# An encoder trunk on one core: the last two up-projection groups of the MLP behind each other, then eight pieces of the down projection

## The chip, the cores and the metric

One core of a Trainium2 chip runs the kernel. The core has TensorE (PE in the profile, with PEld for the loading of weights into it), VectorE (DVE), ScalarE (ACT), GpSimd (POOL) and SyncE (SP), each with its own queue of instructions, which it works off in order. SP issues nearly all DMAs of this kernel. The metric is the device time of one execution in microseconds, as the median over several runs; the profile is of one further execution.

## The reference

Two layers, each with a token mixer and a gated MLP over 256 tokens of width 1024, and a last normalisation. The change touches the MLP alone, whose inner width is 2816, that is 22 chunks of 128 channels:

```python
def _conv_ffn(xn, w_up, conv_w, conv_b, w_down):
    a, gval = jnp.split(xn @ w_up, 2, axis=-1)
    a = lax.conv_general_dilated(a, conv_w[:, None, :], window_strides=(1,),
                                 padding=((CONV_WIDTH // 2, CONV_WIDTH // 2),),
                                 dimension_numbers=('NWC', 'WIO', 'NWC'),
                                 feature_group_count=D_FF) + conv_b
    return (jax.nn.gelu(a) * gval) @ w_down

h = h + _conv_ffn(_rmsnorm(h, norm2[layer]), w_up[layer], conv_w[layer], conv_b[layer], w_down[layer])
```

Branch a is projected, convolved over three tokens for each channel and put through gelu; branch g is projected and multiplied with it; the product goes through the down projection and is added to the residual h.

## The kernel before, in words

**Precision.** Every float32 operand is split into a high and a low part. A weight arrives from memory as a 1 MB load (`raw`, three buffers), and each load holds two pieces. Of each piece ACT makes the high part (`wh`, line 219, a cast) and DVE the low part (`wl`, line 221, a subtraction). A product then takes three matmuls: high by high, high by low, low by high. The class `Weights` hands out the pieces in the order in which they were registered, loads ahead and splits three pieces ahead; `wh` and `wl` have five buffers, so a piece is split only when an older one has been used up by PE.

**The MLP.** Chunks 0 to 19 are projected in groups of four: group `("a", n)` or `("g", n)` is 512 columns of one branch, four pieces, 48 matmuls (`by_tokens`, line 680, tiles `t_ps`). Its result has the tokens on the partitions. `cross` turns it so that the channels lie there: DVE transposes blocks (line 724), SP stores to DRAM (line 726) and reads back with four DMAs (line 731) into `zga` or `zg`. The four reads wait on SP for the store, and what SP has behind them waits too. `z_of` holds two groups of each branch.

`up(f)` finishes a chunk: ACT copies it (line 1277), ACT starts the convolution (1286), DVE adds the two neighbours (1287, 1290), ACT takes gelu (1299), DVE multiplies with branch g (1301), ACT casts the product to the high part `actq` (1310) and DVE subtracts for the low part `actk` (1311). Chunks 20 and 21, the last two, go another way: `proj` (line 556, tiles `proj_ps`) projects them with the channels on the partitions, two pieces at a time, and `add_up` (lines 592, 593) adds the two halves out of PSUM, so that they need no crossing.

**The down projection** (`residual_mm`, lines 598 to 600, tiles `res_ps`) takes one piece of weights and one chunk at a time and adds up in four PSUM tiles. Its last four chunks, 18 to 21, are held: their pieces are fetched but their matmuls run last, output segment by output segment, so that the norm behind can begin on the first segment while the others are still computed. In the last layer (`whole`) the last segment has its residual added ahead, by DVE in line 633.

**The order.** `MLP_STEPS` gives the order of the steps and with it that of the weights: a1, g1, d0, a2, g2, d4, a3, g3, d8, a4, g4, d12, p, d16, d20, behind a0 and g0. Step `("d", n)` is the down projection of four chunks from n on, `("p", 20)` the projection of chunks 20 and 21. `CHUNKS_BEHIND` says which chunks `up` is called for behind each half of a step. Within this order a scheduler places the instructions of each engine as their operands allow, with `issue_after` as a lower bound in some places. `half_steps` runs a step by halves; in step p it calls `up`, which itself calls `proj`.

The tail is thus: p with its two chunks, chunks 17 and 18 behind its first half, chunk 19 behind its second, then d16 and d20, the held matmuls, and behind them the norm of the next layer or the output.

Of the kernel before, what the change touches and what calls it, by code (L numbers as in the profile page):

```python
# [27 lines left out]
NF = DFF // P  # L28
# [10 lines left out]
NQ = NF // 4  # L39


def _mlp_steps():


    steps = []
    for n in range(1, NQ):
        steps += [("a", n), ("g", n), ("d", 4 * n - 4)]
    last = 4 * NQ
    steps.append(("p", last))
    return steps + [("d", f) for f in (last - 4, last)]  # L50


MLP_STEPS = _mlp_steps()
CHUNKS_BEHIND = {
    ("a", 1): ((), (0, 1)), ("g", 1): ((2, 3), ()),
    **{("d", 4 * n): ((), (4 * n + 4,)) for n in range(NQ - 1)},
    **{("a", n): ((4 * n - 3,), (4 * n - 2,)) for n in range(2, NQ)},
    **{("g", n): ((4 * n - 1,), ()) for n in range(2, NQ)},
    ("p", 4 * NQ): ((4 * NQ - 3, 4 * NQ - 2), (4 * NQ - 1,)),
}  # L60
HALVES = (slice(0, 512), slice(512, D))
SEGMENTS = (HALVES, (slice(0, 512), slice(512, 768), slice(768, D)))

# [196 lines left out]
def encoder(ctx, tc, x, w_in, w_pool, pool_scale, w_a, w_b, w_o, norm1, norm2, w_up, conv_w,  # L260
# [13 lines left out]
    def cols(w, c0):  # L274

        src = w[:, c0 : c0 + 256].rearrange("(k p) c -> p k c", p=P)
        return W.add(
            src, (8, 256), [((lambda t, j=j: t[:, :, j * P : (j + 1) * P]), (8, P)) for j in (0, 1)]
        )
# [11 lines left out]
    for l in range(DEPTH):  # L291
        for g in range(NG):
            c0 = C_V + g * 512
            slots = (("m2", 0, 2), ("m2", 1, 2), ("ybig",), ("at2",)) if g == 0 else ()
            for j in range(2):
                tag = "k1" if l == 0 and g == 1 and j == 0 else None
                W.use(rows(w_in[l], j * 512, 4, c0, 512, tag), slots[2 * j : 2 * j + 2])
        if l == 0:
            W.n_scaled = len(W.pieces)
        for c in range(3, -1, -1):  # L300
            W.use(cols(w_in[l], c * 256))
        for n, c in enumerate(PAIRS):
            pool = ([], [])
            if n == 1:
                pool = W.add(
                    w_pool[l].rearrange("g (k p) c -> p (g k) c", p=P), (8, 256),
                    [((lambda t, j=j: t[:, 4 * j : 4 * j + 4, :]), (4, 256)) for j in range(2)],
                )
                pool = (pool[:1], pool[1:])
            W.use(pool[0] + cols(w_in[l], C_Q + c * 256))  # L310
            W.use(pool[1] + cols(w_in[l], C_K + c * 256))
        for w, c0 in ((w_a[l], 0), (w_in[l], C_GP)):
            for c in (c0, c0 + 512):
                W.use(rows(w, 0, 4, c, 512) + rows(w, 512, 4, c, 512))
        for c in (0, 512):
            W.use(rows(w_in[l], 0, 4, C_GA + c, 512) + rows(w_in[l], 512, 4, C_GA + c, 512))
            W.use(rows(w_b[l], 0, 4, c, 512))
        for c in range(4):
            W.use(rows(w_o[l], c * 256))
        first_up.append((len(W.pieces), len(W.loads)))  # L320
        slots = (("v1",), ("ybig",), ("at2",))
        for j in range(2):
            tag = None if j else "k1"
            W.use(rows(w_up[l], j * 512, 4, 0, 512, tag), slots[2 * j : 2 * j + 2])
        for j in range(2):
            W.use(rows(w_up[l], j * 512, 4, DFF, 512))
        for kind, n in MLP_STEPS:
            if kind == "p":
                (a0, a1), (g0, g1) = (cols(w_up[l], c + n * P) for c in (0, DFF))
                W.use([a0, g0, a1, g1])  # L330
            elif kind == "d":
                for f in range(n, min(n + 4, NF), 2):
                    W.use(rows(w_down[l], f * P))
            else:
                for j in range(2):
                    W.use(rows(w_up[l], j * 512, 4, (kind == "g") * DFF + n * 512, 512))
# [227 lines left out]
    def proj(x2, n=1):  # L564


        if not ready:
            pieces = [W.get() for _ in range(n)]
            ps = [mmp.tile([P, 2, S], F32, tag="mm", name="proj_ps") for _ in range(n)]
            two_sums(  # L570
                x2, KD,
                *(
                    (b, lambda k, wh=wh: wh[:, k, :], lambda k, wl=wl: wl[:, k, :])
                    for b, (_, (wh, wl)) in zip(ps, pieces)
                ),
            )
            for i, _ in pieces:
                W.free(i)
            ready.extend((b[:, 0], b[:, 1]) for b in ps)
        return ready.pop(0)  # L580

    def halves(a):

        return a.rearrange("p (t m) -> p t m", t=2)

    def in_order(a):

        return a.rearrange("p (m t) -> p t m", t=2)

    def add_up(out, sums):  # L590

        nc.scalar.copy(out=out, in_=sums[1])
        nc.vector.tensor_add(out=out, in0=sums[0], in1=out)
# [322 lines left out]
    for l in range(DEPTH):  # L916
# [21 lines left out]
        if l == 0:  # L938
            with tc.manual_schedule():
                begun = begin_values_of_x()  # L940
            x2 = first_values(*begun, keep_values)
# [24 lines left out]
        for gi in range(3, -1, -1):  # L966
# [10 lines left out]
            cur, n = u, S + 2 * PAD  # L977
# [108 lines left out]
        def weigh(hh):  # L1086
# [20 lines left out]
        steps = {  # L1107
            0: ((scores, 0), (start_turn, 0)),
            2: ((scores, 1), (start_turn, 1)),
            3: ((turn, 0),),  # L1110
            4: ((weigh, 0),),
            6: ((turn, 1), (scores, 2), (start_turn, 2)),
            7: ((weigh, 1),),
            8: ((scores, 3), (start_turn, 3)),
            12: ((turn, 2),),
# [101 lines left out]
        x2 = two_parts("x", "x2")  # L1217
# [21 lines left out]
            ]  # L1239
            for tag in "qk"  # L1240
        )
        acts = {}

# [27 lines left out]
        def up(f):  # L1273
            w0, w1, w2, b = (prm[:, l, j * NF + f : j * NF + f + 1] for j in range(4))
            a = sm.tile([P, S], F32, tag="u", name="a")
            if f < 4 * NQ:
                nc.scalar.copy(
                    out=a.rearrange("p (a j t) -> p t a j", t=2, j=32),
                    in_=of_chunk(z_of["a", f // 4], f % 4),
                )  # L1280
            else:
                sums = proj(x2, 2)
                with W.after_splits():
                    add_up(in_order(a), [halves(b) for b in sums])
            y = sm.tile([P, S], F32, tag="s", name="y")
            nc.scalar.activation(y, a, AF.Identity, bias=b, scale=w1)  # L1286
            nc.vector.scalar_tensor_tensor(  # L1287
                out=y[:, 1:], in0=a[:, : S - 1], scalar=w0, in1=y[:, 1:], op0=ALU.mult, op1=ALU.add
            )
            nc.vector.scalar_tensor_tensor(  # L1290
                out=y[:, : S - 1], in0=a[:, 1:], scalar=w2, in1=y[:, : S - 1],
                op0=ALU.mult, op1=ALU.add,
            )
            g = sm.tile([P, 2, P], F32, tag="p", bufs=3, name="g")
            if f >= 4 * NQ:
                add_up(g, [halves(a) for a in proj(x2, 2)])

            y2 = sm.tile([P, S], F32, tag="us", name="y2")
            nc.scalar.activation(y2, y, AF.Gelu_apprx_tanh)
            if f < 4 * NQ:  # L1300
                nc.vector.tensor_mul(  # L1301
                    out=g.rearrange("p t (a j) -> p t a j", j=32),
                    in0=y2.rearrange("p (a j t) -> p t a j", t=2, j=32),
                    in1=of_chunk(z_of["g", f // 4], f % 4),
                )
            else:
                nc.vector.tensor_mul(out=g, in0=in_order(y2), in1=g)
            n = f % NH
            ah, al = (x[n >= HPG][:, n - HPG * (n >= HPG)] for x in (acth, actl))
            nc.scalar.copy(out=ah, in_=g)  # L1310
            nc.vector.tensor_sub(out=al, in0=g, in1=ah.bitcast(F32))  # L1311
            acts[f] = (ah, al)
# [16 lines left out]
        def half_steps(kind, n):  # L1329
            if kind == "p":  # L1330
                for f in (n, n + 1):
                    up(f)
                    yield
            elif kind == "d":
                for _ in range(n, min(n + 4, NF), 2):
                    next(down)
                    next(down)
                    yield
            else:
                yield from by_halves(kind, n)  # L1340

        for at in MLP_STEPS:
            if at[0] == "d" and at[1] == 4 * NQ:
                break
            chunks = CHUNKS_BEHIND.get(at, ((), ()))
            for _, some in zip(half_steps(*at), chunks):
                for f in some:
                    up(f)
        if l + 1 < DEPTH:
            x2 = two_parts("x", "x2")  # L1350
# [34 lines left out]
```

## Time and profile before

| what | value |
|---|---|
| median of three runs | 870.12 us (869.45 to 870.21) |
| profiled execution | 872.57 us |
| its span, from first to last instruction | 870.8 us |
| PE busy | 856.6 us, 98% |
| PEld, DVE, ACT busy | 724.2, 619.9, 492.3 us |
| DMA moved | 195.17 MB, mean 224 GB/s |

A row of the timeline gives the start in us from the span's start, the duration, the engine, the line, the operation, the tiles (out<-in), the shape and a count; in brackets stands the idle time ahead of it and what ended it. Matmuls are pipelined: a row of 0.39 us is the way of one matmul through the array, and what it costs is the distance to the next start. A row of the waits gives who waited for whom, the sum in us, the number of times and the longest. A row of the groups gives the count, the busy time in all and the mean of one in ns, then the idle time before. Lines are those of the kernel before.

### The profile page before, as it was taken

What the parts mean: (1) busy time and instruction counts of PE and PEld (TensorE: products, weight loads), DVE (VectorE), ACT (ScalarE), POOL (GpSimd) and SP (SyncE); (2) the same over time, 40 slices, a digit from 0 to 9 for tenths busy, and PEclk for the clock granted to TensorE, in tenths of its full rate; (3) what the DMA queues carried; (4) which work ended last, traced back from release to release, by engine and by line L of the source; (5) the groups of instructions that cost most, each with busy time, mean ns of one, the idle gap of its engine ahead of it and who ended that gap; (6) DMA issues with size and microseconds to landing.
All of it is one profiled execution on the core that took longest, in us unless ns stands there. A gap on an engine that the chain in (4) does not pass through costs nothing.

```text
span 870.8 us, 11486 instructions
## 1 busy us (share of the span) xinstructions
PE 856.6 (98%) x4215; PEld 724.2 (83%) x4215; DVE 619.9 (71%) x930; ACT 492.3 (57%) x770; POOL 34.5 (4%) x98
## 2 busy tenths in 40 slices
PE   9999999999999999999899999999999999999996
PEld 8888888888888888888688888988888888888874
DVE  7998785557676777675865987765666777767664
ACT  7656575555455646555645676664544466646462
POOL 1800000000010000000000000000000000000000
PEclk9999999999999999999999999999999999999998
DMA  9676566775736788696626565747875578778631
GB/s 337 205 251 199 189 201 212 265 257 197 267 124 227 257 268 312 221 323 213 233 97 218 170 215 177 240 143 248 307 238 196 165 271 274 268 263 295 228 145 48
DMA packets 139071, 195.17 MB, mean 224 GB/s; under 512 B 6200, under 2 KB 80640, under 8 KB 139016
## 3 DMA queue, kind: packets, MB, share of 16 engines
q1 hardware_dynamic: 138856, 194.18, 65.9%
q8 instruction: 33, 0.54, 0.2%
q10 hardware_dynamic: 160, 0.27, 0.1%
q14 instruction: 22, 0.18, 0.1%
HBM read 176.58 MB, written 17.85 MB: 223 GB/s over the span
## 4 chain that ended last, share of the span: by engine, by line
PE 91%; DVE 3%; DMA 3%; ACT 2%; issue 1%; SPq 0%; POOL 0%; POOLq 0%; ACTq 0%
PE t_ps L680 38%; PE proj_ps L556 22%; PE v_ps L680 6%; PE res_ps L598 5%; PE res_ps L600 5%; PE res_ps L599 5%; PE v_ps L908 3%; DVE wl L221 2%; PE v_ps L815 1%; PE pool_ps L556 1%; DMA crossing<-crossing 1%; PE o_ps L1096 1%; PE s_ps L1047 1%; DMA raw<-in_w_up_dram 1%; PE s_ps L1042 1%; PE o_ps L1092 1%
## 5 line engine op out<-in xcount | busy, mean ns | idle before, releaser
L221 DVE TENSOR_TENSOR wl<-raw,wh 128x1024 fp32r<-128x1024 f32 x274 | 330.2, 1220 | 134.7 <-ACT wh L219 117.7
L219 ACT CAST wh<-raw 128x1024 fp32r<-128x1024 f32 x274 | 283.1, 1049 | 142.1 <-PE t_ps L680 81.5
L680 PE MATMUL t_ps<-wh,x 128*128 128x512 f32 x832 | 259.0, 390 | 0.0
L680 PEld LDWEIGHTS t_ps<-wh,x 128*128 128x128 f32 x832 | 156.2, 188 | 32.3
L680 PE MATMUL t_ps<-wl,x 128*128 128x512 f32 x416 | 161.9, 389 | 0.1
L556 PE MATMUL proj_ps<-x,wh 128*128 128x512 f32 x576 | 136.5, 390 | 0.0
L556 PEld LDWEIGHTS proj_ps<-x,wh 128*128 128x128 f32 x576 | 106.6, 188 | 21.2
L680 PEld LDWEIGHTS t_ps<-wl,x 128*128 128x128 f32 x416 | 78.1, 188 | 16.7 <-DVE wl L221 0.5
L598 PE MATMUL res_ps<-wh,actq 128*128 128x512 f32 (+1 forms) x184 | 71.1, 395 | 7.1 <-ACT actq L1310 4.4
L556 PE MATMUL proj_ps<-x,wl 128*128 128x256 f32 x576 | 74.9, 283 | 0.0
L556 PEld LDWEIGHTS proj_ps<-x,wl 128*128 128x128 f32 x576 | 72.8, 191 | 1.9
L599 PE MATMUL res_ps<-wl,actq 128*128 128x512 f32 (+1 forms) x184 | 71.7, 390 | 0.0
L600 PE MATMUL res_ps<-wh,actk 128*128 128x512 f32 (+1 forms) x184 | 71.0, 390 | 0.0
L598 PEld LDWEIGHTS res_ps<-wh,actq 128*128 128x128 f32 x184 | 35.6, 194 | 16.1 <-ACT actq L1310 6.3
L600 PEld LDWEIGHTS res_ps<-wh,actk 128*128 128x128 f32 x184 | 35.6, 194 | 7.4 <-DVE actk L1311 0.2
L599 PEld LDWEIGHTS res_ps<-wl,actq 128*128 128x128 f32 x184 | 35.7, 194 | 6.9
L680 PE MATMUL t_ps<-wh,po 128*128 128x512 f32 x128 | 41.4, 395 | 0.0
L1310 ACT CAST actq<-g 128x256 fp32r<-128x256 f32 x44 | 17.4, 400 | 29.7 <-DVE g L1301 28.3
L468 POOL TENSOR_SCALAR ss<-ss 128x1 f32<-128x1 f32 x8 | 1.9, 238 | 792.4 <-ACT junk L461 792.4
L724 DVE STREAM_TRANSPOSE crossing<-t_ps 128x512 f32<-128x512 f32 x36 | 24.4, 701 | 9.8 <-PE t_ps L680 9.8
L1287 DVE SCALAR_TENSOR_TENSOR y<-a,prm,y 128x255 f32<-128x255 f32 x44 | 20.6, 477 | 11.0 <-ACT y L1286 11.0
L680 PEld LDWEIGHTS t_ps<-wh,po 128*128 128x128 f32 x128 | 24.0, 188 | 4.9
(203 smaller groups left out, 1080.6 us busy)
## 6 DMA issues: line engine op xcount, KB each, us to landing
raw<-in_w_in_dram SPq DMA_DIRECT2D x58, 1024.0 KB, 5.8
raw<-in_w_up_dram SPq DMA_DIRECT2D x44, 1024.0 KB, 5.3
raw<-in_w_down_dram SPq DMA_DIRECT2D x22, 1024.0 KB, 5.3
crossing<-crossing SPq DMA_DIRECT2D x20, 512.0 KB, 4.8
raw<-in_w_a_dram SPq DMA_DIRECT2D x8, 1024.0 KB, 6.1
raw<-in_w_o_dram SPq DMA_DIRECT2D x8, 1024.0 KB, 4.7
zga<-crossing SPq DMA_DIRECT2D x40, 128.0 KB, 2.6
zg<-crossing SPq DMA_DIRECT2D x40, 128.0 KB, 2.7
```

Of the source, the lines that this page charges most:

```text
L219: inst = nc.scalar.copy(out=h, in_=src)
L221: inst = nc.vector.tensor_sub(out=l, in0=src, in1=h.bitcast(F32))
L556: nc.tensor.matmul(out, w(k), x, start=(steps is first and k == 0), stop=(steps is last and k == nk - 1), skip_group_check=turns["rest"],)
L598: nc.tensor.matmul(ps, ah, wh, start=first, stop=False, skip_group_check=on)
L599: nc.tensor.matmul(ps, ah, wl, start=False, stop=False, skip_group_check=on)
L600: nc.tensor.matmul(ps, al, wh, start=False, stop=last, skip_group_check=on)
L680: nc.tensor.matmul(ps, x2[:, 2 * n + j, part, t, :], w[:, j, :], start=(n + m == 0), stop=(n == last and m == 5),)
L724: nc.vector.transpose(out=y[:, t].rearrange("p q c j -> p c q j"), in_=rows[t])
L815: return nc.tensor.matmul(ps[t], a[:, k, t, :], w[:, k % 2, :], start=first, stop=last)
L908: nc.tensor.matmul(ps[t], a[:, k, t, :], w[:, j, :], start=(k + m == 0), stop=(k == KD - 1 and m == 2),)
L1287: nc.vector.scalar_tensor_tensor(out=y[:, 1:], in0=a[:, : S - 1], scalar=w0, in1=y[:, 1:], op0=ALU.mult, op1=ALU.add)
L1310: nc.scalar.copy(out=ah, in_=g)
```

## The change

The list of steps is written out, each with the chunks behind its two halves. Step d8 moves from between g3 and a4 to behind g4, so a3, g3, a4 and g4 run directly behind each other, and d8 and d12, eight pieces of the down projection, follow. The chunks keep their ascending order, and now the last two come last: 12 behind a4, 13 and 14 with g4, 15 and 16 with d8, 17 and 18 with d12, 19 and 20 behind the first half of p and 21 behind its second. For that, the projection of chunks 20 and 21 is taken out of `up`: step p computes `sums[f]` (two tiles of PSUM for each chunk), and `up` reads them later. All else, the number of instructions of each kind among it, stays.

```diff
-MLP_STEPS = _mlp_steps()
-CHUNKS_BEHIND = {
-    ("a", 1): ((), (0, 1)), ("g", 1): ((2, 3), ()),
-    **{("d", 4 * n): ((), (4 * n + 4,)) for n in range(NQ - 1)},
-    **{("a", n): ((4 * n - 3,), (4 * n - 2,)) for n in range(2, NQ)},
-    **{("g", n): ((4 * n - 1,), ()) for n in range(2, NQ)},
-    ("p", 4 * NQ): ((4 * NQ - 3, 4 * NQ - 2), (4 * NQ - 1,)),
-}
+MLP_STEPS = (
+    ("a", 1, ((), (0, 1))), ("g", 1, ((2, 3), ())),
+    ("d", 0, ((), (4,))), ("a", 2, ((5,), (6,))), ("g", 2, ((7,), ())),
+    ("d", 4, ((), (8,))), ("a", 3, ((9,), (10,))), ("g", 3, ((11,), ())),
+    ("a", 4, ((), (12,))), ("g", 4, ((13,), (14,))),
+    ("d", 8, ((15,), (16,))), ("d", 12, ((17,), (18,))),
+    ("p", 20, ((19, 20), (21,))), ("d", 16, None), ("d", 20, None),
+)
...
             else:
-                sums = proj(x2, 2)
                 with W.after_splits():
-                    add_up(in_order(a), [halves(b) for b in sums])
+                    add_up(in_order(a), [halves(b) for b in sums[f][0]])
...
             if f >= 4 * NQ:
-                add_up(g, [halves(a) for a in proj(x2, 2)])
+                add_up(g, [halves(b) for b in sums[f][1]])
...
             if kind == "p":
                 for f in (n, n + 1):
-                    up(f)
+                    sums[f] = proj(x2, 2), proj(x2, 2)
                     yield
...
-        for at in MLP_STEPS:
-            if at[0] == "d" and at[1] == 4 * NQ:
+        for kind, n, chunks in MLP_STEPS:
+            if chunks is None:
                 break
-            chunks = CHUNKS_BEHIND.get(at, ((), ()))
-            for _, some in zip(half_steps(*at), chunks):
+            for _, some in zip(half_steps(kind, n), chunks):
                 for f in some:
                     up(f)
```

More of the change, by code (lines that the diff above doesn't have):

```diff
@@ L39 @@
 NQ = NF // 4
[L42 to L50, printed above, removed]
-MLP_STEPS = _mlp_steps()
-CHUNKS_BEHIND = {
-    ("a", 1): ((), (0, 1)), ("g", 1): ((2, 3), ()),
-    **{("d", 4 * n): ((), (4 * n + 4,)) for n in range(NQ - 1)},
-    **{("a", n): ((4 * n - 3,), (4 * n - 2,)) for n in range(2, NQ)},
-    **{("g", n): ((4 * n - 1,), ()) for n in range(2, NQ)},
-    ("p", 4 * NQ): ((4 * NQ - 3, 4 * NQ - 2), (4 * NQ - 1,)),
-}
+MLP_STEPS = (
[6 rows of a table added]
+)
 HALVES = (slice(0, 512), slice(512, D))
@@ L326, in encoder @@
             W.use(rows(w_up[l], j * 512, 4, DFF, 512))
-        for kind, n in MLP_STEPS:
+        for kind, n, _ in MLP_STEPS:
             if kind == "p":
@@ L1241, in encoder @@
         )
-        acts = {}
+        acts, sums = {}, {}
         zg = big.tile([P, 2, 8, 4, 32], F32, tag="v1", name="zg")
@@ L1331, in half_steps @@
                 for f in (n, n + 1):
-                    up(f)
+                    sums[f] = proj(x2, 2), proj(x2, 2)
                     yield
             elif kind == "d":
-                for _ in range(n, min(n + 4, NF), 2):
+                for _ in range(2):
                     next(down)
```

## The prediction

> **What bounds the kernel now.** I read the page first, then PE's waits, then PE's instructions in order of time in the two places where it waits.
>
> ```profile
> span 870.8 us, 11486 instructions
> PE 856.6 (98%) x4215; PEld 724.2 (83%) x4215; DVE 619.9 (71%) x930; ACT 492.3 (57%) x770; POOL 34.5 (4%) x98
> ```
>
> PE is busy for 98% of the span, so nothing but its own holes and its own clock can be won. The change leaves the matmuls as they are. The waits say where the holes lie:
>
> ```profile
> PE res_ps L598 <- ACT actq L1310: 4.4, 5, 3.1
> PE res_ps L598 <- DVE res_ps L633: 2.6, 1, 2.6
> ```
>
> These 7.0 us are the down projection waiting for the last chunks' activations (L1310) and, in the last layer, for a DVE add (L633) queued behind them. PE's timeline, the tail of the first layer and then of the last:
>
> ```profile
> 414.70 0.39 PE L600 MATMUL res_ps<-wh,actk 128*128 128x512 f32 x1
> 415.44 0.50 PE L598 MATMUL res_ps<-wh,actq 128*128 128x512 f32 x1 [0.34 <-ACT actq L1310]
> ...
> 418.11 0.40 PE L600 MATMUL res_ps<-wh,actk 128*128 128x512 f32 x1
> 418.81 0.50 PE L598 MATMUL res_ps<-wh,actq 128*128 128x512 f32 x1 [0.30 <-ACT actq L1310]
> ...
> 421.25 0.28 PE L600 MATMUL res_ps<-wh,actk 128*128 128x256 f32 x1
> 424.59 0.50 PE L598 MATMUL res_ps<-wh,actq 128*128 128x512 f32 x1 [3.06 <-ACT actq L1310]
> ```
>
> ```profile
> 843.43 0.39 PE L600 MATMUL res_ps<-wh,actk 128*128 128x512 f32 x1
> 844.16 0.50 PE L598 MATMUL res_ps<-wh,actq 128*128 128x512 f32 x1 [0.34 <-ACT actq L1310]
> ...
> 846.78 0.39 PE L600 MATMUL res_ps<-wh,actk 128*128 128x512 f32 x1
> 847.54 0.50 PE L598 MATMUL res_ps<-wh,actq 128*128 128x512 f32 x1 [0.37 <-ACT actq L1310]
> ...
> 849.03 0.89 PE L600 MATMUL res_ps<-wh,actk 128*128 128x512 f32 x3
> 852.57 1.01 PE L598 MATMUL res_ps<-wh,actq 128*128 128x256 f32 x2 [2.64 <-DVE res_ps L633]
> ```
>
> Each long hole is followed by matmuls at a lower granted clock (the columns of the windows are the stretch, its length, busy time of PE, PEld, DVE, ACT, POOL, granted clock, DMA share, GB/s):
>
> ```profile
> 424.60:429.00 4.40, 4.40 (x12) 3.48 (x13) 4.12 (x5) 1.94 (x2) 0.00 (x0) 0.61 0.97 310
> 852.50:859.10 6.60, 6.53 (x16) 5.21 (x17) 1.82 (x4) 0.83 (x3) 0.22 (x1) 0.52 0.00 0
> ```
>
> The undisturbed pace is read from the chain of waits:
>
> ```profile
> 259.37 21.77 PE t_ps L680 x96
> ...
> 335.96 21.76 PE t_ps L680 x96
> 368.60 21.76 PE t_ps L680 x96
> 401.24 5.57 PE proj_ps L556 x32
> ```
>
> 96 matmuls in 21.76 us are 0.227 us each; one piece of weights (12 matmuls) takes 2.72, one group of a branch (4 pieces) 10.9. A 256-column matmul takes half, 0.12.
>
> **What the holes cost.** From start to start, less the pace. First layer: 0.74 - 0.23 = 0.51; 0.70 - 0.23 = 0.47; 3.34 - 0.12 = 3.22; then 12 matmuls in 4.40 instead of 2.72, 1.68. Together 5.9 us. Last layer: 0.50; 0.53; 3.54 - 0.68 = 2.86; then 14 matmuls of 512 and two of 256 in 6.60 instead of 3.41, 3.2. Together 7.1 us. All 13.0 us come from one cause: ACT and DVE do five chunks (20, 17, 18, 21, 19) while PE has only eight pieces' worth of matmuls to run, the four of step p and d16's two, before it asks for 18 to 21.
>
> The page of the Trainium skill "TensorE: Matmul & The Clock Gate" (section "What's actually happening") says that after an idle window of about 3.4 us the array runs at half rate until it has been busy for one such window. By it each long hole would cost an estimated 1.7 us of slow matmuls, 3.4 in all, and the forecast would end 1.5 us higher; here holes of 3.06 and of only 2.64 us brought the clock down to 0.61 and 0.52, and the slow stretch cost 1.7 once and 3.2 once, so the rows decide.
>
> **The change, part by part.** In each layer the 48 matmuls of d8, with four casts, four subtractions and two 1 MB loads, go behind groups a4 and g4. PE's sum is unchanged. POOL sees nothing. On SP the two loads move past the two loads each of a4 and g4 and past g3's issues; a4's crossing (one store, four reads back) now follows g3's by one group, not two, and d8's and d12's loads stand between or behind the crossings.
>
> Chunks: as built, the queues of ACT and DVE take chunks 12 to 15 as one batch during a4 and g4, 16 to 19 as one batch during d8 and d12. So 17, 18 and 19, which are now done during p and d16, are finished before p begins, hidden beside eight pieces of matmuls (21.8 us). Only 20 and 21 are left for p and the tail.
>
> Tail, counted from p's start, by these group rows of the page:
>
> ```profile
> L221 DVE TENSOR_TENSOR wl<-raw,wh 128x1024 fp32r<-128x1024 f32 x274 | 330.2, 1220 | 134.7 <-ACT wh L219 117.7
> L219 ACT CAST wh<-raw 128x1024 fp32r<-128x1024 f32 x274 | 283.1, 1049 | 142.1 <-PE t_ps L680 81.5
> ...
> L1310 ACT CAST actq<-g 128x256 fp32r<-128x256 f32 x44 | 17.4, 400 | 29.7 <-DVE g L1301 28.3
> ...
> L1287 DVE SCALAR_TENSOR_TENSOR y<-a,prm,y 128x255 f32<-128x255 f32 x44 | 20.6, 477 | 11.0 <-ACT y L1286 11.0
> ```
>
> PE runs p until 11.1 (four projections: each pair 5.57, the chain's row), piece 16 until 13.9, 17 until 16.6, then three matmuls each of 18, 19, 20, and asks for chunk 21 at 16.6 + 3 x 0.68 = 18.6. DVE's queue, from its add of chunk 20 at about 6.6 (below) to the low half of chunk 21: five subtractions (17 to 21) x 1.22, four convolution steps x 0.48, eight smaller ones (four adds, two products, two low halves) x 0.40: 6.1 + 1.9 + 3.2 = 11.2, so 17.8. ACT: the cast of piece 21 waits for piece 16's buffer (13.9), then 1.05 + 0.4 (gelu) + 1.05 (first layer only: the cast of the next weights stands ahead) + 0.4 = 16.8. Chunk 21 is 0.8 us early; L633 follows at 18.2 and is not asked for until the last segments. So the holes go, and with them the slow clock. What is late next is chunk 21, by this margin.
>
> Terms that before does not show at this place: four crossings in a row. But the start of the same layer has them (a0, g0, a1, g1, then d0), with the same batches of four chunks. SP's timeline there, first layer and then two rows of the last:
>
> ```profile
> 281.91 0.37 SPq L726 DMA_DIRECT2D crossing<-crossing  x1
> 291.99 1.81 SPq L731 DMA_DIRECT2D zga<-crossing  x4
> ...
> 295.28 0.37 SPq L726 DMA_DIRECT2D crossing<-crossing  x1
> 303.74 2.27 SPq L731 DMA_DIRECT2D zg<-crossing  x4
> 306.11 0.94 SPq L155 DMA_DIRECT2D raw<-in_w_up_dram  x2
> ...
> 711.07 0.37 SPq L726 DMA_DIRECT2D crossing<-crossing  x1
> ...
> 732.52 0.95 SPq L155 DMA_DIRECT2D raw<-in_w_up_dram  x2
> ```
>
> SP stands 10.1 and 8.5 us until each crossing lands, and the weight loads queued behind stand with it. ACT gets these loads so, and PE waited for them once:
>
> ```profile
> 311.96 2.00 ACT L219 CAST wh<-raw 128x1024 fp32r<-128x1024 f32 x2 [0.91 <-DMA raw<-in_w_up_dram]
> 314.52 2.00 ACT L219 CAST wh<-raw 128x1024 fp32r<-128x1024 f32 x2 [0.56 <-DMA raw<-in_w_up_dram]
> 316.98 2.00 ACT L219 CAST wh<-raw 128x1024 fp32r<-128x1024 f32 x2 [0.46 <-PE t_ps L680]
> ```
> ```profile
> PEld t_ps L680 <- DVE wl L221: 0.5, 1, 0.5
> ```
>
> Copied to the new place: a1 ended at 259.37 + 21.77 = 281.1, a4 will end at 368.6, 87.5 later. The loads of p then go at 393.6, p starts at 401.1, its first piece is cast from 399.4, the second (other load) from 402.0 to 403.05, asked for after 8 matmuls at 402.9: 0.2 us of waiting. Casts of p's other two follow until 405.1, piece 16's until 406.2, piece 17's until 407.3 behind the buffer that PE frees, chunk 20's copy by 407.7: DVE's add at p + 6.6. In the last layer the loads came 24.2 - 21.45 = 2.7 us sooner behind the crossing: nothing. Bounds for this term: none, or, were each of the two crossings as slow as the slower one, 2 x 1.6 less 0.3 of margin, 2.9 us a layer. I take 0.2, the row of the same pattern.
>
> Into the next layer: PE ends 5.9 us earlier, but the load behind piece 21's subtraction only by some 5, and its cast stands ahead of the norm's squares on ACT.
>
> ```profile
> 427.94 1.05 ACT L219 CAST wh<-raw 128x1024 fp32r<-128x1024 f32 x1 [2.45 <-DMA raw<-in_w_in_dram]
> 429.46 0.63 ACT L461 ACTIVATE junk<-h 128x512 f32<-128x512 f32 x1 [0.48 <-DVE h L459]
> ```
>
> Now that cast ends at 429.0, 0.5 ahead of the first square; moved by 5 against 5.9 it delays the squares by 0.4. Bounds: 0, or 2 if the load is as late as ACT's wait there. I take 0.4.
>
> Sum: 5.9 + 7.1 - 0.2 - 0.4 = 12.4 us off. The profiled execution took 872.57 us (span 870.8); it would show a span of 858.4. The median, 870.12, lies 2.45 below the profiled execution; the same 12.4 off it gives 857.7 us.
>
> **Rivals.** (A) Chunk 21 stays late in the first layer: its cast stands behind the cast of a freshly loaded piece.
>
> ```profile
> raw<-in_w_in_dram SPq DMA_DIRECT2D x58, 1024.0 KB, 5.8
> ```
>
> For: the margin is 0.8 us, and that load leaves when piece 17 is split (6.6 + 2 x 0.4 + 1.22 = 8.6), 6.8 us ahead of the cast at 15.4, of which 5.8 go into landing. Against: both margins hold by these rows. If the old third hole comes back with its slow clock, 3.2 + 1.7: 862.6.
>
> (B) p starves: crossings land late and p's loads with them. A hole of 2.9 with a slow clock of 1.7 to 3.2, about 5 a layer: 862.7 in one layer, 867.7 in both. For: the bound above. Against: in the same pattern PE waited 0.5 us.
>
> (C) Slower. SP's round becomes the bound: 281.91 to 295.28 is 13.4 us from crossing to crossing where PE needs 10.9 per group. If a4, g4, d8 and d12 each inherit this 2.5 us, the three pieces split ahead (8.2 us) are used up by p; with two holes of 2.5 and their slow clock (2.5) before p and a third at p, a layer loses 15, both 30, less 12.4: 888. It decides from 6.5 us lost per layer on. Against: a0 to g1 show the round once and PE's 96 matmuls at pace. The page "DMA: Bandwidth & Descriptors" (section "Anatomy of one DMA") states that a wait on a semaphore is spent on the issuing sequencer; SP's 10.1 us ahead of the reads agree, and this is the rule that speaks against four crossings in a row.
>
> (D) The tail is as long as before because PE waits for 20 and 21 as it did for 19: 870.
>
> **Numbers.** Forecast 55%, A 15, B 11 (one layer) and 6 (both), C 10, D 3. The forecast's own range is 856.5 (no new costs, less rounding) to 860; with A and B in one layer to 866, so that B in both and C and D, 19%, are left out: 856.5 to 866. 0.2%, 1.7 us, is about what a measurement here can tell. Faster 0.87, same 0.03, slower 0.10.
>
> **What would show it.** PE's waits should lose both L598 rows (5 times from ACT, once from L633), and the windows over both tails should hold clock 1.00. Chunks 16 to 19 should end before p begins. A PE wait at the first proj_ps matmuls of p means B; at t_ps of g4 or res_ps of d8, C; a wait for the L1310 cast of chunk 21 with the next weights' cast ahead of it, A. It is wrong if PE's wait in total stays above 4 us.

## The result, and the profile after

The changed kernel takes 858.52 us (median of 4 runs, 857.52 to 860.33), the kernel before, run beside it, 869.79 us (4 runs, 868.91 to 870.21). The ratio is 0.9874, with a 95% interval of 0.9855 to 0.9893: 11.3 us, or 1.3%, are gone. The profiled execution took 858.57 us with a span of 856.8; against the span of before, 870.8, that is 14.0 us.

The first rows of the page of the changed kernel, and behind them its complete list of PE's waits (us in total, times, longest):

```profile
span 856.8 us, 11482 instructions
PE 850.0 (99%) x4215; PEld 721.3 (84%) x4215; DVE 620.7 (72%) x930; ACT 492.1 (57%) x770; POOL 34.4 (4%) x98
```

```profile
PE gain_ps L375 <- PEq L1354: 0.8, 1, 0.8
PE xt_ps L752 <- DMA h<-in_x_dram: 0.3, 1, 0.3
```

Both rows of the down projection have gone (its line is now 587); what is left lies at the very start of the program. DVE, ACT and POOL have the busy times of before within 1 us, so their work was not saved, only placed. Windows in the two tails (columns as in the prediction) hold clock 1.00, and PE is busy throughout; over the whole first tail (401.1 to 429.6) and in the last one from 841 to 850 the same view gives 1.00 and a busy PE too:

```profile
424.60:429.00 4.40, 4.40 (x34) 4.06 (x33) 2.42 (x6) 1.78 (x7) 1.00 (x4) 1.00 0.78 303
823.00:841.00 18.00, 18.00 (x96) 15.54 (x95) 14.04 (x21) 10.40 (x17) 0.00 (x0) 1.00 0.32 117
```

Where the time went is read from three starts on PE's timeline: p of the first layer, the next layer's first `v_ps`, p of the last layer. Before:

```profile
401.08 1.98 PE L556 MATMUL proj_ps<-x,wh 128*128 128x512 f32 x8
...
436.15 3.00 PE L680 MATMUL v_ps<-m,x 128*128 128x512 f32 x12
...
829.80 1.98 PE L556 MATMUL proj_ps<-x,wh 128*128 128x512 f32 x8
```

After:

```profile
401.11 3.79 PE L545 MATMUL proj_ps<-x,wh 128*128 128x512 f32 x16
...
429.58 3.15 PE L669 MATMUL v_ps<-m,x 128*128 128x512 f32 x12
...
823.34 3.79 PE L545 MATMUL proj_ps<-x,wh 128*128 128x512 f32 x16
```

Up to p nothing has moved (401.08, 401.11). The first tail, p to `v_ps`, fell from 35.07 to 28.47 us, by 6.6; the stretch between the tails is 393.7 and 393.8; the last tail, p to the end of the span, fell from 41.0 to 33.5, by 7.5. These two lengths are the measure for all experiments below; each is the difference of two such rows, or of one and the span:

| kernel | first tail, us | last tail, us | span, us | median, us |
|---|---|---|---|---|
| before | 35.07 | 41.0 | 870.8 | 869.79 |
| after | 28.47 | 33.5 | 856.8 | 858.52 |
| e1: d8 not moved | 34.26 | 36.9 | 865.2 | 867.23 |
| e2: moved, chunk 20 first | 31.22 | 33.8 | 859.4 | 860.41 |
| e3: before, holes filled | 33.69 | 38.2 | 868.0 | 867.93 |
| e5: six crossings in a row | 28.86 | 33.5 | 858.0 | 860.02 |
| e6: e1, g's copies behind the casts | 29.58 | 33.5 | 857.6 | 859.25 |
| e7: before, g's copies behind the casts | 35.60 | 38.6 | 868.4 | 870.81 |
| e4: after, chunk 21 later by 4 | 29.27 | 33.5 | 856.8 | 858.82 |
| e4: after, chunk 21 later by 12 | 32.39 | 33.8 | 860.5 | 862.16 |

### The profile page after: what moved, and what is told of

Same layout as the page of the kernel before. It is cut to its first block, busy times and chain, and to the rows that moved or that the text cites. A ratio compares the mean times of both kernels' runs of the same rounds, so it can differ in the third digit from the quotient of the medians.

```text
span 856.8 us, 11482 instructions
## 1 busy us (share of the span) xinstructions
PE 850.0 (99%) x4215; PEld 721.3 (84%) x4215; DVE 620.7 (72%) x930; ACT 492.1 (57%) x770; POOL 34.4 (4%) x98
## 4 chain that ended last, share of the span: by engine, by line
PE 99%; DMA 1%; ACT 0%; SPq 0%; POOLq 0%; issue 0%; POOL 0%; ACTq 0%
PE t_ps L669 41%; PE proj_ps L545 23%; PE v_ps L669 6%; PE res_ps L589 6%; PE res_ps L587 6%; PE res_ps L588 6%; PE v_ps L897 3%; PE pool_ps L545 1%; PE v_ps L804 1%; PE o_ps L1085 1%; PE s_ps L1036 1%; PE s_ps L1031 1%; PE o_ps L1081 1%; PE xt_ps L484 1%; DMA h<-in_x_dram 1%; PE xt_ps L752 0%
## 5 line engine op out<-in xcount | busy, mean ns | idle before, releaser
L588 PE MATMUL res_ps<-wl,actq 128*128 128x512 f32 (+1 forms) x184 | 69.9, 380 | 0.0
L587 PE MATMUL res_ps<-wh,actq 128*128 128x512 f32 (+1 forms) x184 | 67.7, 380 | 0.0
L713 DVE STREAM_TRANSPOSE crossing<-t_ps 128x512 f32<-128x512 f32 x36 | 24.5, 702 | 11.1 <-PE t_ps L669 11.0
L1275 DVE SCALAR_TENSOR_TENSOR y<-a,prm,y 128x255 f32<-128x255 f32 x44 | 20.8, 477 | 11.6 <-ACT y L1274 11.3
```

The source lines that it names most:

```text
L587: nc.tensor.matmul(ps, ah, wh, start=first, stop=False, skip_group_check=on)
L588: nc.tensor.matmul(ps, ah, wl, start=False, stop=False, skip_group_check=on)
L713: nc.vector.transpose(out=y[:, t].rearrange("p q c j -> p c q j"), in_=rows[t])
L1275: nc.vector.scalar_tensor_tensor(out=y[:, 1:], in0=a[:, : S - 1], scalar=w0, in1=y[:, 1:], op0=ALU.mult, op1=ALU.add)
```

## The experiments

The kernel before took 869.24 us (19 runs) beside e1, e2, e3 and e5, and 868.58 us (13 runs) beside e6, e7 and the two of e4; ratios are against these.

### e1: the order of the chunks without the move of d8

```diff
-    ("a", 4, ((), (12,))), ("g", 4, ((13,), (14,))),
-    ("d", 8, ((15,), (16,))), ("d", 12, ((17,), (18,))),
-    ("p", 20, ((19, 20), (21,))), ("d", 16, None), ("d", 20, None),
+    ("d", 8, ((), (12,))), ("a", 4, ((13,), (14,))), ("g", 4, ((15,), ())),
+    ("d", 12, ((), (16,))),
+    ("p", 20, ((17, 18, 19, 20), (21,))), ("d", 16, None), ("d", 20, None),
```

> The changed kernel with d8 back between g3 and a4; chunks 17 to 19 are finished behind the first half of p again, but ahead of 20, and 21 stays last with its projection done apart. Theory (what matters is how many chunks ACT and DVE still have to finish once p's projections run): the branch g of chunks 16 to 19 lands at about p's start less 2 us, as in the kernel before, their products take some 3.3 us, so 17 to 19 are done at p's start plus 1 to 2, and 20 and 21 follow as in the changed kernel, about 1 us later against a margin of 1.3 us. So 10 to 13 of the 13 us stay, the time is 857 to 861 us. Rival (the eight pieces of the down projection behind g4 are what hides 17 to 19): the tail does five chunks again, holes of 3 us and slow clock in both layers, 866 to 871 us.

Measured: 867.23 us (10 runs), ratio 0.9981 (0.9966 to 0.9996). The gain was not kept; my theory missed. PE's waits show that it is not the old holes that came back. PE hardly waits for activations any more but for weights, `wh` and `wl`, and once for the norm's `xn`:

```profile
PE res_ps L587 <- ACT wh L208: 2.8, 2, 1.4
PE xt_ps L484 <- DVE xn L475: 2.2, 1, 2.2
PE res_ps L588 <- DVE wl L210: 1.7, 4, 0.5
```

Why ACT was late with them stands in its timeline during p of the first layer (p begins at 400.45):

```profile
401.86 0.40 ACT L1298 CAST actq<-g 128x256 fp32r<-128x256 f32 x1
406.21 0.37 ACT L581 COPY g<-proj_ps 128x256 f32<-128x256 f32 x1 [3.96 <-PE proj_ps L545]
406.48 0.41 ACT L1298 CAST actq<-g 128x256 fp32r<-128x256 f32 x1
411.78 0.37 ACT L581 COPY g<-proj_ps 128x256 f32<-128x256 f32 x1 [4.89 <-PE proj_ps L545]
412.05 1.05 ACT L208 CAST wh<-raw 128x1024 fp32r<-128x1024 f32 x1
```

By 402.3 chunks 16 to 18 have left ACT. Then it stands, 3.96 and 4.89 us, at the copies of branch g of chunks 20 and 21, whose matmuls have not run yet. Chunk 19's last cast (406.48) stands behind the first of them, and the cast of the first piece of d16 behind the second, until 412.05, 11.6 us into p. So this run differs from the changed kernel in two things, the place of d8 and the order in which the scheduler put these copies on ACT. In `add_up` for branch a the copy is held behind the latest weight cast (`after_splits`); for branch g it is not. e6 takes the two apart.

### e6: e1, with branch g's copies behind the casts

```diff
-                add_up(g, [halves(b) for b in sums[f][1]])
+                with W.after_splits():
+                    add_up(g, [halves(b) for b in sums[f][1]])
```

> The kernel with d8 left in its old place (and all chunks 17 to 20 behind the first half of p) once more, with one thing added: the two copies of branch g of chunks 20 and 21 out of PSUM may not stand ahead of the latest weight cast on ACT, as those of branch a may not already. In the run without this, ACT stood 3.96 and 4.89 us at the head of its queue for these two copies while the cast of piece 16 waited behind them. Theory 1 (what counts is that chunks 16 to 19 are done before p and that ACT can split weights during p; where d8 stands does not matter): the holes go, 857 to 861 us. Theory 2 (the move of d8 is needed, since only eight pieces in a row behind g4 give the cover): the holes stay, 865 to 868 us.

Measured: 859.25 us (4 runs), ratio 0.9899 (0.9874 to 0.9924). One line brings back 7 us (by the ratios) to 8 us (by the medians), with d8 in its old place: theory 1 holds, theory 2 falls. ACT in the same stretch (p begins at 400.91):

```profile
402.97 0.41 ACT L1299 CAST actq<-g 128x256 fp32r<-128x256 f32 x1 [0.26 <-DVE g L1290]
403.29 1.05 ACT L208 CAST wh<-raw 128x1024 fp32r<-128x1024 f32 x1
405.71 0.39 ACT L581 COPY a<-proj_ps 128x256 f32<-128x256 f32 x1 [1.38 <-PE proj_ps L545]
406.72 0.37 ACT L581 COPY g<-proj_ps 128x256 f32<-128x256 f32 x1 [0.63 <-PE proj_ps L545]
406.99 1.06 ACT L208 CAST wh<-raw 128x1024 fp32r<-128x1024 f32 x1
```

The cast of d16's first piece (403.29) now runs 2.4 us into p and not 11.6, and of the tails' waits only one of 1.0 us for the norm's `xn` is left. Chunk 19 leaves ACT at 403.4, 2.5 us into p: in this point theory 1 was too strict, the chunks need not be done before p, only ahead of chunk 20 in the queues.

### e7: the kernel before, with branch g's copies behind the casts

The kernel before has such a wait too, 7.22 us in its first tail (ACT's timeline, p begins at 401.08):

```profile
406.84 0.37 ACT L592 COPY g<-proj_ps 128x256 f32<-128x256 f32 x1 [7.22 <-PE proj_ps L556]
```

This run holds the copies back there, and nothing else.

```diff
-                add_up(g, [halves(a) for a in proj(x2, 2)])
+                gate = proj(x2, 2)
+                with W.after_splits():
+                    add_up(g, [halves(a) for a in gate])
```

> The kernel before with only this: the two copies of branch g of chunks 20 and 21 may not stand ahead of the latest weight cast on ACT. In the kernel before ACT stands 7.2 us at such a copy in each layer. Theory 1 (five chunks in too little time; the wait of ACT at the head of its queue is a part of it, but chunk 17 stays behind chunk 20's copies in any case): one cast of 1.05 us moves ahead of the wait and the long hole shrinks by about 1 us a layer, 866 to 868.5 us. Rival (the wait at the copy is all of the cause): with it gone the holes go too, 857 to 861 us.

Measured: 870.81 us (10 runs), ratio 1.0021 (1.0005 to 1.0036): no gain but a loss of 2 us, so the wait at the copy alone is not the cause. The size of theory 1, a gain of about 1 us a layer, was missed as well. PE's waits in the tails, and ACT in the first tail (p begins at 400.54):

```profile
PE res_ps L598 <- ACT actq L1312: 4.1, 1, 4.1
PE res_ps L598 <- DVE res_ps L633: 2.3, 1, 2.3
```

```profile
401.01 1.05 ACT L219 CAST wh<-raw 128x1024 fp32r<-128x1024 f32 x1
405.34 0.39 ACT L592 COPY a<-proj_ps 128x256 f32<-128x256 f32 x1 [3.28 <-PE proj_ps L556]
406.30 0.37 ACT L592 COPY g<-proj_ps 128x256 f32<-128x256 f32 x1 [0.57 <-PE proj_ps L556]
406.56 0.44 ACT L1277 COPY a<-zga 128x256 f32<-128x256 f32 x1
```

The cast has moved ahead, but chunk 17 (line 1277) still begins at 406.56, behind both copies of chunk 20, although its input came with the same crossing as that of chunk 16, whose last cast ended on ACT at 401.1. The two short holes and the long one of each layer have become one: 4.14 us in the first tail, where the three had 3.70 together, and 2.28 in the last, where they had 3.35. So neither the chunks' order alone (e1) nor the copies behind the casts alone (e7) brings the gain, both together (e6) do. e6 also has the projections of chunks 20 and 21 taken out of `up`, as in the changed kernel; no run separates this from the order.

### e2: the move of d8 without the new order of chunk 20

Chunk 20 comes first in p again, its projections inside `up` as before, then 19 and 21.

```diff
-    ("p", 20, ((19, 20), (21,))), ("d", 16, None), ("d", 20, None),
+    ("p", 20, ((), (19,))), ("d", 16, None), ("d", 20, None),
...
+                own = proj(x2, 2)
-                    add_up(in_order(a), [halves(b) for b in sums[f][0]])
+                    add_up(in_order(a), [halves(b) for b in own])
...
-                add_up(g, [halves(b) for b in sums[f][1]])
+                add_up(g, [halves(b) for b in proj(x2, 2)])
...
-                    sums[f] = proj(x2, 2), proj(x2, 2)
+                    up(f)
```

> The changed kernel with d8 behind g4, but chunk 20 finished first in p with its own projection, then 19, then 21, as the kernel before orders them. Theory: 16 to 18 are done before p, three chunks are left for the tail and not five, each 1.8 us of DVE; the last is chunk 19 or 21, at most 2 us later than in the changed kernel against 1.3 us of margin: 858 to 861 us. Rival (the order of the last chunks, the one with the projections last, is what counts): the hole of chunk 19 stays with its slow clock, 5 us a layer, 866 to 870 us.

Measured: 860.41 us (4 runs), ratio 0.9899 (0.9884 to 0.9915), as expected. PE's waits:

```profile
PE xt_ps L484 <- DVE xn L475: 0.7, 1, 0.7
PE proj_ps L545 <- ACT wh L208: 0.7, 1, 0.7
PE res_ps L587 <- ACT actq L1299: 0.6, 1, 0.6
```

So there are two ways to most of the gain: the move of d8, by which chunks 17 and 18 stand ahead of chunk 20 (e2; the two copies of branch g had no wait of ACT ahead of them in its first tail), or the new order of the chunks with ACT kept free (e6). The change has the move and the order together.

### e3: the kernel before, with its long hole filled

Fourteen matmuls of 512 columns into a scratch tile stand ahead of chunk 21's or 19's held matmuls, in each layer; their result is not used.

```diff
+        if n == NF:
+            scratch = mmp.tile([P, 512], F32, tag="mm", name="busy_ps")
+            (_, (ah, al, wh, wl)) = held[0]
+            for _ in range(14):
+                nc.tensor.matmul(scratch, ah[:, 0], wh[:, 0, 0:512], start=True, stop=True)
```

> The kernel before with 14 further matmuls of 512 columns (3.2 us at pace), a product of chunk 18 into a PSUM tile that nobody reads, ahead of the held matmuls of the down projection in each layer; its result is the reference's. The holes stay filled with work of no use. If the low granted clock (0.61 and 0.52) comes from PE being idle for 2.6 to 3.1 us, the slow stretches go and 1.7 + 3.2 us with them: 4 to 5 us less than the kernel before, 865 us. If the clock falls for another reason (the kind of matmul, or the place), nothing is won: 870 us, or up to 3 us more.

Measured: 867.93 us (10 runs), ratio 0.9981 (0.9968 to 0.9994). The waits for L633 and the long one for `actq` are gone, and the stretch that ran at 0.52 in the last layer of the kernel before (852.50 to 859.10) now holds 1.00:

```profile
852.90:859.40 6.50, 6.50 (x32) 5.44 (x31) 2.90 (x5) 1.45 (x4) 0.70 (x3) 1.00 0.00 0
```

In all ten runs the mean granted clock was 0.998 or more, in 14 of the 19 of the kernel before it was 0.997 or less. That idle time is what brings the clock down is thereby shown. Between the two profiles the two tails are 4.1 us shorter (35.07 and 41.0 against 33.69 and 38.2), about as expected. But the median won only 1.3 us, not the 4 to 5. The runs of the kernel before beside it say why: they differ in the main by their slow stretches. Of the 19 runs, the five with a mean granted clock of 0.998 took 867.39 to 867.94 us, those with 0.996 to 0.997 took 868.79 to 869.32 (six) and 870.90 to 871.47 (three), and the five with 0.993 to 0.994 took 870.54 to 872.32. (The three slow ones at 0.996 show that something else, worth 2 us, varies too; no run here says what.) The filled kernel is as fast as the first five. The execution that I had the profile of was one with slow stretches in both tails; by the clocks the median has an estimated third of that.

### e5: six crossings in a row

```diff
-    ("d", 0, ((), (4,))), ("a", 2, ((5,), (6,))), ("g", 2, ((7,), ())),
-    ("d", 4, ((), (8,))), ("a", 3, ((9,), (10,))), ("g", 3, ((11,), ())),
+    ("a", 2, ((), (4,))), ("g", 2, ((5,), (6,))),
+    ("d", 0, ((7,), (8,))), ("d", 4, ((9,), (10,))),
+    ("a", 3, ((11,), ())), ("g", 3, ((), ())),
```

Here a0, g0, a1, g1, a2, g2 come directly behind each other, before any piece of the down projection.

> The changed kernel with the order a1, g1, a2, g2, d0, d4, a3, g3, a4, g4, d8, d12: with a0 and g0 ahead, six groups and six crossings in a row, then four. If the lookahead of the weights absorbs SP's round of 13.4 us for six groups as it did for four, the time is that of the changed kernel within 2 us. If SP's round is the bound of such a row (rival C of the prediction), each further group comes 2.5 us late: 5 us a layer, and with holes over 2.5 us a slow clock of 1.7 to 3.2 us more: 868 to 875 us.

Measured: 860.02 us (4 runs, 859.64 to 864.45), ratio 0.9907 (0.9879 to 0.9934), within 2 us of the changed kernel as the first theory has it. SP's stores and reads in that stretch of the first layer:

```profile
282.73 0.37 SPq L716 DMA_DIRECT2D crossing<-crossing  x1
288.18 1.81 SPq L721 DMA_DIRECT2D zga<-crossing  x4
...
304.49 0.37 SPq L716 DMA_DIRECT2D crossing<-crossing  x1
314.62 1.81 SPq L721 DMA_DIRECT2D zga<-crossing  x4
...
317.99 0.42 SPq L716 DMA_DIRECT2D crossing<-crossing  x1
```

From the fifth crossing of the run to the sixth, 304.49 to 317.99, is a round of 13.5 us, as long as the one that rival C rested on. Yet PE does not wait at all there; in the last layer it waits once, 0.22 us, for a `wl`, behind the last of the six. The two rounds before this one, from 282.73 to 304.49, take 21.8 us, PE's own pace for two groups, and none of the last layer's five rounds takes more than 11.6. The one longer round must have been paid from the pieces that are split ahead; I have not followed them one by one.

### e4: chunk 21 later, by four and by twelve DVE instructions

```diff
+            if f == NF - 1:
+                for _ in range(4):
+                    nc.vector.tensor_scalar_mul(y, y, 1.0)
```

The other kernel has 12 in the place of 4.

> The changed kernel with four more DVE instructions on chunk 21 (multiplication by 1.0, some 0.5 us each, 2.0 us in all) between its convolution and its gelu. Theory (chunk 21 has about 1.2 us of slack ahead of its gelu, which waits for a weight cast on ACT, and 1.26 us ahead of PE's first use): it stays hidden, 857.5 to 859.5 us. Rival (chunk 21 is on the path already): 2 us a layer more, 862 to 863 us.

> The changed kernel with twelve more such DVE instructions on chunk 21, 6.1 us in all. Theory (some 2.5 us are hidden, the rest is a hole of about 3.5 us in each layer): 865 us if the clock stays up, 869 to 872 us if each hole is followed by a slow stretch of 1.7 to 3.2 us as in the kernel before; its runs then differ with the granted clock. Rival (everything behind DVE moves with it): 12 us, 870 to 871 us without any slow clock.

Measured: 858.82 us (4 runs), ratio 0.9889 (0.9872 to 0.9906), and 862.16 us (4 runs), ratio 0.9930 (0.9912 to 0.9948). Four cost nothing, as expected: the first tail is 0.8 us longer, but p began 0.7 us sooner, and the span is the same. Twelve cost 3.3 us more than four, not 6 to 13. Two rows of PE and one of DVE from the kernel with twelve, first layer:

```profile
425.98 0.50 PE L587 MATMUL res_ps<-wh,actq 128*128 128x512 f32 x1 [1.37 <-ACT actq L1301]
430.84 0.41 PE L484 MATMUL xt_ps<-ident,xn 128*128 128x128 f32 x2 [2.17 <-DVE xn L475]
```

```profile
422.97 1.61 DVE L1284 TENSOR_SCALAR y<-y 128x256 f32<-128x256 f32 x5
```

My size was wrong first: five take 1.61 us, 0.32 each and not 0.5, so twelve are 3.9 us. Then the scheduler answered: in both kernels it put the matmuls of chunks 18 to 20 of the later output segments ahead of chunk 21's, so with twelve chunk 21 was asked for 25.3 us into p (400.71 to 425.98) and not 18.6. The last layer then lost 0.3 us, the first 3.9. The margin of 0.8 us that I had worked out for a fixed order of PE was therefore not tested as such; what the runs show is that the scheduler makes room when it knows of the delay. The clock stayed at 1.00 behind the hole of 1.37 us, and behind that of 2.17 us too (1.00 up to 436).

## Why the prediction was right

**The forecast.** 857.7 us were predicted, 858.5 measured. The mechanism was right: the holes of both tails went, and the slow clock with them. The number is closer than its terms deserve, and that is luck, since errors of opposite sign stood in it.

**First layer's tail, 5.9 less 0.2 and 0.4.** Measured 6.6. All three holes and the slow stretch are gone. The 0.2 at p's start did not come: p's loads left SP at 391.7, not 393.6, since the crossings ahead of them landed sooner (SP stood 8.8 and 8.6 us at them, against the 10.1 and 8.5 of the row that was copied), and PE ran from 401.11 without a wait. (e2 has this wait, 0.65 us at p's second piece, so the mechanism exists.) The 0.4 at the norm came on ACT but not on PE: the weight cast ahead of the squares ends at 424.3, 4.7 earlier than before, and holds the first square back by 0.6 behind DVE's add; PE has held matmuls of the other segments to run meanwhile and does not wait for `xn`. The other 0.7 us are small delays of PE in the kernel before that the prediction left out, by its rows from start to start against the pace: 0.36 at the norm (a matmul waits for `xn` at 433.90), 0.1 for the first matmul behind each of the two short holes, the rest spread.

**Last layer's tail, 7.1.** Measured 7.5; 0.2 of the difference are again the first matmuls behind the two short holes.

**The sum against the median.** Here a step failed: "the same 12.4 off it gives 857.7". Of the 12.4, 4.9 were slow clock (1.7 and 3.2), and these are not in every run of the kernel before, as e3 and the runs beside it show: the median, 869.24, has about 1.5 us of it above the 867.7 of the runs that have least. Holes of 8.1 us, an estimated 1.5 of slow clock and the 1.1 us by which the two tails gained more than their terms (0.7 and 0.4) make 10.7; 11.3 were measured. The gain in the profiled execution was underrated by 1.6 (14.0 against 12.4), that in the median overrated by 1.1, and the median of before came out 0.3 lower: 857.7 + 1.1 - 0.3 = 858.5.

**Chunk 21.** Its low half was to be ready at p + 17.8, against a demand at p + 18.6. ACT's and DVE's timelines of the changed kernel:

```profile
400.25 4.85 ACT L208 CAST wh<-raw 128x1024 fp32r<-128x1024 f32 x5 [2.08 <-DMA raw<-in_w_up_dram]
...
406.85 0.37 ACT L581 COPY g<-proj_ps 128x256 f32<-128x256 f32 x1 [0.57 <-PE proj_ps L545]
...
412.42 0.37 ACT L581 COPY g<-proj_ps 128x256 f32<-128x256 f32 x1 [0.49 <-PE proj_ps L545]
...
416.42 1.04 ACT L208 CAST m<-raw 128x1024 fp32r<-128x1024 f32 x1
417.36 0.40 ACT L1298 CAST actq<-g 128x256 fp32r<-128x256 f32 x1
```

```profile
396.23 0.98 DVE L1299 TENSOR_TENSOR actk<-g,actq 128x256 fp32r<-128x256 f32 x2
...
406.31 0.42 DVE L582 TENSOR_TENSOR a<-proj_ps,a 128x256 f32<-128x256 f32 x1 [0.35 <-ACT a L581]
...
418.02 0.42 DVE L1299 TENSOR_TENSOR actk<-g,actq 128x256 fp32r<-128x256 f32 x1
```

Chunks 16 to 19 are done at 397.2, before p, as said. DVE's add of chunk 20 comes at p + 5.2, not 6.6, because p's pieces were cast sooner (400.25). Chunk 21 is ready at 418.44, p + 17.3. The next weights' cast does stand ahead of its own cast (416.42), as rival A had it, and it fits.

**The cause.** "All 13.0 us come from one cause", five chunks on ACT and DVE beside "only eight pieces' worth of matmuls", was too short. (The four pieces of p and d16's two are six and not eight; the working below it, with 16.6 us until PE asks for chunk 18, has it right.) Of that time ACT stood 7.2 us at a copy of p's result (the row shown with e7), with chunks 17 to 19 and a weight cast behind it. I had read PE's timeline in the tail, not ACT's in p. It follows that the move of d8, on which the prediction builds its cover of "eight pieces of matmuls (21.8 us)", is sufficient for most of the gain (e2) but not necessary (e6). And the changed kernel has luck in it: its copies of branch g at 406.85 and 412.42 make ACT wait only 0.57 and 0.49 us, because the scheduler put the casts of d16's first two pieces ahead of them (among the five from 400.25 on). Nothing in the edit asks for that, and in e1 the same code got the other order.

**The rivals.** A: the chain that it feared is there but ends 1.26 us early. B: no wait at p. C: no wait of PE in the changed kernel, and in e5 six crossings in a row cost 0.2 us of waiting; the one round of 13.5 us came behind four of 10.1 to 11.1. D: falls with the waits.

## What to carry to other kernels

When an engine waits for the results of others at the end of a stage, read the queues of those others as well: an instruction at the head of ACT's queue that waits for matmuls not yet run stops everything behind it (4.89 us at one copy in e1), and putting ready work ahead of it (e6) was worth nearly as much as moving a step with 2 MB of weights in each layer. A wait taken away alone can merge with the next (e7); here the order of the queue had to change with it. And a profiled execution can hold costs, such as a slow clock, that only some runs have; set the sum against several runs and their clocks before taking it off the median.

## What the runs showed of the hardware

In these traces the clock falls to half (0.50), in stretches of about 3.4 us or twice that, and a hole of 2.3 us can be enough. Windows of half a microsecond in the last tail of the kernel before:

```profile
851.50:852.00 0.50, 0.00 (x0) 0.00 (x0) 0.50 (x3) 0.00 (x0) 0.00 (x0) 0.97 0.00 0
852.00:852.50 0.50, 0.00 (x0) 0.00 (x0) 0.50 (x2) 0.29 (x1) 0.00 (x0) 0.50 0.00 0
...
858.00:858.50 0.50, 0.50 (x3) 0.33 (x1) 0.45 (x1) 0.50 (x2) 0.00 (x0) 0.50 0.00 0
858.50:859.00 0.50, 0.50 (x3) 0.46 (x2) 0.00 (x0) 0.04 (x1) 0.22 (x1) 0.70 0.00 0
```

The last matmul ended at 849.92 (the row of three at 849.03 in the prediction); the clock fell at 851.97, 2.05 us later and inside the hole, and rose at 858.8, 6.8 us on. (A window of 0.5 us at 0.70 has 0.3 us at half and then 0.2 at full clock.) In the first tail it fell at 425.3 (0.81 from 425.0 to 425.5), when PE had been running again for 0.7 us, and rose at 428.7 (0.78 from 428.5 to 429.0). In e7 it behaved in the same way around its holes of 4.1 and 2.3 us:

```profile
424.00:424.50 0.50, 0.50 (x2) 0.17 (x2) 0.50 (x3) 0.00 (x0) 0.00 (x0) 0.80 1.06 414
...
427.50:428.00 0.50, 0.50 (x4) 0.38 (x3) 0.06 (x1) 0.00 (x0) 0.00 (x0) 0.79 1.03 401
850.50:851.00 0.50, 0.09 (x1) 0.09 (x1) 0.50 (x3) 0.45 (x2) 0.00 (x0) 0.97 0.00 0
...
854.00:854.50 0.50, 0.50 (x3) 0.39 (x2) 0.00 (x0) 0.00 (x0) 0.00 (x0) 0.62 0.00 0
```

The clock of each window gives the instant: 424.3 to 427.7 and 850.97 to 854.4, 3.4 us both times. With its holes merged, e7 had a clock of 0.992 to 0.994 in nine of ten runs, and the kernel before that low in three of the 13 runs beside it. So whether a hole of 2.3 to 3.1 us brings the clock down differs from run to run; the waits of 2.17 us in e1 and e4 had clock 1.00 behind them. The Trainium skill's page "TensorE: Matmul & The Clock Gate" (section "What's actually happening") has a free-running window of about 3.4 us and half rate; the length and the rate agree, and a free-running window would explain the spread from run to run. It has the clock fall after at least one idle window; here it fell 2.05 us after the last matmul, so the measurement decides against that. What exactly the gate counts, no run here shows.
